# A transformer block: VectorE's weight splits queued behind the copies that TensorE waits for, and latent attention in another order

## The chip, the cores and the metric

One core of a Trainium2 chip (trn2). Five engines work from queues of their own: TensorE (PE: matmuls and transposes into PSUM), VectorE (DVE), ScalarE (ACT), GpSimd (POOL) and SyncE (SP, which here issues the transfers of the weights). An engine takes its queue strictly in order, so an instruction that waits holds up all that stand behind it on its engine. The metric is the device time of one execution in microseconds: the median of three is 914.4 us (912.42 to 914.48).

## The reference, cut to what matters

Two blocks on 256 tokens of width 1024, all in float32. The first has a layer with a bidirectional mLSTM beside spatial gating, and a layer with latent attention. Each is followed by a feed-forward layer of width 4096. The second block has chunked attention and SwiGLU. The part that is re-ordered is the latent attention:

```python
    cq, ckv, kr = jnp.split(h @ w_in, [Q_LORA, Q_LORA + KV_LORA], axis=-1)       # 384, 256, 32
    q = (rms_norm(cq, q_g) @ w_uq).reshape(bsz, seq, C_HEADS, C_NOPE + C_ROPE)   # 16 heads of 64 + 32
    kv = (rms_norm(ckv, kv_g) @ w_ukv).reshape(bsz, seq, C_HEADS, C_NOPE + C_V)  # 64 + 64
    q_rope = apply_rope(q[..., C_NOPE:], cos, sin)
    k_rope = apply_rope(kr[:, :, None, :], cos, sin)
    ...
    s = jnp.einsum("bqhd,bkhd->bhqk", qblk, kf) * scale
    pr = jax.nn.softmax(s, axis=-1)
    o = jnp.einsum("bhqk,bkhd->bqhd", pr, v)
    return o @ w_out
```

The outer parts are `x + ab_mixer(...)` and `x + mla_mixer(...)`, each followed by `x + square(relu(rms_norm(x) @ w1)) @ w2`.

## The kernel before, in words

**Products.** TensorE works on a reduced float32 type (fp32r), and each float32 factor is split into a high and a low part. A product of 128x128 weights with 128x256 activations takes three matmuls (`three`, L369 to L374): high weight by high activation (L371), high weight by low activation (L372), low weight by high activation (L373).

**The weight stream.** Weights arrive as chunks of up to 128x2048 (1 MB), listed in `items` in order of use. `Stream` transfers them into a ring of three `raw` buffers. For each chunk ScalarE writes the high part `whi` (L149), and VectorE, or GpSimd for the chunks named in `ON_POOL`, writes the low part `wlo = raw - whi` (L152), mostly in two halves of 128x1024. Four pairs `whi`/`wlo` are held. These steps are put into the program a few at a time between matmuls, by a list of deferred work (`Later`), and a scheduler then settles the order of each engine's queue. `issue_after(x)` tells it that an instruction has to stand behind x; no wait on the chip comes with it. `S.behind` already uses this for `whi` on ScalarE.

**Activations.** A finished sum is added into `head`, the residual (L497). ScalarE rounds it to `xh`, VectorE forms `xl` (L303), and the next layer's matmuls need both.

**Latent attention (L900 to L1202).** In this stretch TensorE's order is the order of the code. The latents `ch`/`cl` (`cl`: L949) are projected by `q_rope` (rotary parts of the queries, 18 matmuls), `q_nope` (L1006 copies the result to `qn`, 18 matmuls), `k_nope` (L1011 scales it into `kn`, 12 matmuls) and `values` (6 matmuls of 128x512, ScalarE writes `v`, L1023). The 16 heads are worked in four groups. `sc(a)` makes the scores of four heads (L1071, L1076). `exps(a)` takes their maxima on VectorE (L1086, L1087), and ScalarE exponentiates in two pairs of heads, with the row sums (L1090). `nrm(j)` takes reciprocals (L1097) and scales one head of the pair on VectorE, the other on GpSimd (L1100). `tr(j)` transposes a pair on TensorE (L1114), copied to `pT` (L1116). `pv(j)` multiplies by the values (L1126). Projections, transposes (j up to 3) and `pv` results share one ring of four PSUM banks (`mmt`); the scores have another (`auxt`). A product can start only when the bank it gets, used four products earlier, has been read. Then follows `c_out`, the output projection.

Of the kernel before, what the change touches and what calls it, by code (L numbers as in the profile page):

```python
# [10 lines left out]
F32 = mybir.dt.float32  # L11
# [39 lines left out]
def spread(ap, axis, n):  # L51

    shape = list(ap.shape)
    shape[axis] = n
    return ap.broadcast_to(shape)
# [44 lines left out]
class Stream:  # L100
# [4 lines left out]

    def __init__(self, tc, later, raw_pool, hl_pool, items, on_pool=()):
        nc = tc.nc
        self.tc, self.behind = tc, None
        self.on_pool = set(on_pool)
        self.nc, self.later, self.raw_pool, self.hl_pool, self.items = nc, later, raw_pool, hl_pool, items  # L110
        self.raw, self.hl, self.todo = {}, {}, {}
        self.n_dma = self.n_split = self.n_use = self.n_plan = 0
# [18 lines left out]
    def split(self):  # L131

        i = self.n_split
        if i >= len(self.items):
            return
        self.n_split += 1
        w = self.items[i].shape[-1]
        r = self.raw.pop(i)
        hi = self.hl_pool.tile([P, BLK * P], F32R, tag="whi", name="whi")
        lo = self.hl_pool.tile([P, BLK * P], F32R, tag="wlo", name="wlo")  # L140
        self.hl[i] = (hi, lo)
        n = self.parts(i)
        parts = [slice(j * w // n, (j + 1) * w // n) for j in range(n)]

        eng = self.nc.gpsimd if i in self.on_pool else self.nc.vector

        def h(s):
            with self.tc.issue_after(self.behind.ins) if self.behind else nullcontext():
                self.nc.scalar.activation(hi[:, s], r[:, s], AF.Copy)  # L149

        def l(s, last):
            eng.tensor_tensor(lo[:, s], r[:, s], hi[:, s].bitcast(F32), op=ALU.subtract)  # L152
            if last:
                self.dma()

        steps = []
        for n, s in enumerate(parts):
            steps.append(lambda s=s: h(s))
            steps.append(lambda s=s, last=n == len(parts) - 1: l(s, last))
        self.todo[i] = steps  # L160
# [33 lines left out]
def block_kernel(ctx, tc, a, out):  # L194
# [46 lines left out]
    items = []  # L241
    on_pool = []
    for n in ("w_va", "w_qk01", "w_qk23", "w_vb", "w_u", "w_oa", "w_ab_out", "w1_0", "w2_0", "w_cin",
              "w_uq", "w_uk", "w_uv", "w_uq2", "w_c_out", "w1_1", "w2_1", "w_qk2", "w_v2",
              "w_o2", "w_gu4", "w_gu", "w_down"):
        first = len(items)
        items += [a[n][i] for i in range(a[n].shape[0])]
        if n == "w_cin":
            items[-1] = items[-1][:, 0:KB * P]
        on_pool += [first + i for i in ON_POOL.get(n, ())]  # L250
# [49 lines left out]
    def split_x(k, src, scale):  # L300

        act.activation(xh[:, k], src, AF.Copy, scale=scale)
        dve.scalar_tensor_tensor(xl[:, k], src, scale, xh[:, k].bitcast(F32), op0=ALU.mult,  # L303
                                 op1=ALU.subtract)

    def split_lo(k, g):
        dve.scalar_tensor_tensor(xl[:, k], x[:, k], col(g, k), xh[:, k].bitcast(F32), op0=ALU.mult,
# [590 lines left out]
    with tc.tile_pool(name="mla", bufs=1) as ap:  # L898
# [43 lines left out]
        def c_evac(m, ps):  # L942
            for i in range(ps.shape[1]):
                j = m + i
                kv = j < 2
                g = col("kv_g", j) if kv else col("q_g", j - 2)
                sq = tmp.tile([P, T], F32, tag="sq", name="sq", bufs=3)
                act.activation(ch[:, j], ps[:, i], AF.Copy, scale=g)
                dve.scalar_tensor_tensor(cl[:, j], ps[:, i], g, ch[:, j].bitcast(F32), op0=ALU.mult,  # L949
                                         op1=ALU.subtract)  # L950
                act.activation(sq, ps[:, i], AF.Square)
                key = "kv" if kv else "q"
                if j in (0, 2):
                    state[key] = sq
                else:
                    n = mp.tile([P, T], F32, tag="sqa", name="sqa", bufs=2)
                    pool.tensor_tensor(n, state[key], sq, op=ALU.add)
                    state[key] = n
                if j == 1:
                    later(4.4, rkv_chain)  # L960
                if j == 4:
                    later(6.0, rq_chain)
# [18 lines left out]
        def tiles(w, b0, h, l, nk, n):  # L981

            ps = mmt().rearrange("p (a b) -> p a b", a=2)
            wh, wl = w
            for i in range(n):
                for k in range(nk):
                    s = slice((b0 + i * nk + k) * P, (b0 + i * nk + k + 1) * P)
                    three(ps[:, i], wh[:, s], wl[:, s], h[k], l[k], k == 0, k == nk - 1)
            return ps
# [3 lines left out]
        def q_rope(w, g):  # L993

            ps = tiles(w, 6 * g, CK[2:5], CL[2:5], 3, 2)
            qs = qr[:, 2 * g:2 * g + 2]
            q2 = mp.tile([P, 2, T], F32, tag="q2", name="q2")
            act.activation(qs, ps, AF.Copy)
            for i in range(2):
                dve.stream_shuffle(q2[:, i], qs[:, i], SHUF)  # L1000
                pool.tensor_tensor(qs[:, i], qs[:, i], cosT, op=ALU.mult)
                dve.tensor_tensor(q2[:, i], q2[:, i], sinT, op=ALU.mult)
                dve.tensor_tensor(qs[:, i], qs[:, i], q2[:, i], op=ALU.add)

        def q_nope(w, g):
            dve.tensor_copy(qn[g], tiles(w, 6 * (g % 2), CK[2:5], CL[2:5], 3, 2))  # L1006

        def k_nope(w, g):
            ps = tiles(w, 4 * g, CK[0:2], CL[0:2], 2, 2)
            for i in range(2):  # L1010
                dve.tensor_tensor(kn[g][:, i], ps[:, i], rbc[1], op=ALU.mult)  # L1011

        def values(w, n, tt):
            ts = slice(tt * P, (tt + 1) * P)
# [27 lines left out]
        act.activation(kr4, thin(wkr, "c_norm"), AF.Copy)  # L1042

        w = S.get()
        q_rope(w, 0)
        key_rope()
        q_rope(w, 1)
# [2 lines left out]
        q_nope(w, 0)  # L1050
        wk = S.get()
        k_nope(wk, 0)
        q_nope(w, 1)
        S.done(held=2)
        k_nope(wk, 1)
        wv = S.get()
        later.flush()
        mpc.__exit__(None, None, None)
        mpc = tc.tile_pool(name="mls", bufs=2)
# [20 lines left out]
        def exps(a, pss):  # L1080
            for p in range(2):
                mx = mp.tile([P, 2, 2], F32, tag="mx", name="mx", bufs=3)
                sm = mp.tile([P, 2, 2], F32, tag="sm", name="sm", bufs=8)
                prs = [mp.tile([P, 2, T], F32, tag="pr", name="pr", bufs=16) for _ in range(2)]
                for i in range(2):
                    dve.tensor_reduce(mx[:, i], pss[2 * p + i], axis=AX, op=ALU.max)  # L1086
                dve.tensor_tensor(mx, mx, spread(nsrq.unsqueeze(1), 1, 2), op=ALU.mult)  # L1087
                for i in range(2):
                    for qt in range(2):
                        S.behind = act.activation(prs[i][:, qt], pss[2 * p + i][:, qt], AF.Exp,  # L1090
                                                  scale=srq[:, qt:qt + 1], bias=mx[:, i, qt:qt + 1],
                                                  accum_out=sm[:, i, qt:qt + 1])
                st_p[2 * a + p] = (prs, sm)

        def nrm(j):
            prs, sm = st_p[j]
            dve.reciprocal(sm, sm)  # L1097
            for i in range(2):
                for qt in range(2):
                    (pool if i else dve).tensor_scalar(prs[i][:, qt], prs[i][:, qt], sm[:, i, qt:qt + 1], None,  # L1100
                                                       op0=ALU.mult)
# [5 lines left out]
        def tr(j):  # L1107
            prs, sm = st_p.pop(j)
            st_t[j] = []
            for i in range(2):  # L1110
                ps = bank(j).rearrange("p (a b) -> p a b", a=2)
                for kt in range(2):
                    for qt in range(2):
                        pe.transpose(ps[:, kt, qt * P:(qt + 1) * P], prs[i][:, qt, kt * P:(kt + 1) * P], ident)  # L1114
                pT = pT_[(2 * j + i) % 4]
                (act.activation(pT, ps, AF.Copy) if i and j > 3 else dve.tensor_copy(pT, ps))  # L1116
                st_t[j].append(pT)
            later.tick(0.9)

# [17 lines left out]
            dve.tensor_tensor(yl[j], o[:, 0:T], yh[j].bitcast(F32), op=ALU.subtract)  # L1137

        sc(0)
        w = S.get()  # L1140
        q_nope(w, 2)
        k_nope(wk, 2)
        values(wv, 0, 0)
        values(wv, 0, 1)
        nrm(0)
        nrm(1)
        sc(1)
        q_nope(w, 3)
        S.done(held=3)
        k_nope(wk, 3)  # L1150
        S.done(held=2)
        values(wv, 1, 0)
        values(wv, 1, 1)
        S.done()
        nrm(2)
        nrm(3)
        sc(2)
        tr(0)
        tr(1)
        pv(0)  # L1160
        tr(2)
        pv(1)
        nrm(4)
        nrm(5)
        sc(3)
        tr(3)
        pv(2)
        pv(3)
        nrm(6)
        nrm(7)  # L1170
# [455 lines left out]
```

## Time and profile before

| What | Value |
|---|---|
| median of three runs | 914.4 us (912.42 to 914.48) |
| the profiled execution | 912.91 us, of which the span from first to last instruction is 911.2 us |
| TensorE busy | 881.4 us, 97% of the span, 6744 matmuls |
| VectorE, ScalarE, GpSimd busy | 578.1, 470.7, 277.1 us |
| chain that ended last | TensorE 83%, VectorE 9% (its L152 alone 3%) |
| mean granted clock of TensorE | 0.986 of full speed |

TensorE is the bound almost everywhere, so an edit matters only where it changes TensorE's idle time or its clock. The list of waits says what TensorE stood idle for; the timeline of an engine says what it did then; the table by stretches shows its clock (1.00 is 2.4 GHz, 0.50 is 1.2 GHz).

### The profile page before, as it was taken

What the parts mean: (1) busy time and instruction counts of PE and PEld (TensorE: products, weight loads), DVE (VectorE), ACT (ScalarE), POOL (GpSimd) and SP (SyncE); (2) the same over time, 40 slices, a digit from 0 to 9 for tenths busy, and PEclk for the clock granted to TensorE, in tenths of its full rate; (3) what the DMA queues carried; (4) which work ended last, traced back from release to release, by engine and by line L of the source; (5) the groups of instructions that cost most, each with busy time, mean ns of one, the idle gap of its engine ahead of it and who ended that gap; (6) DMA issues with size and microseconds to landing.
All of it is one profiled execution on the core that took longest, in us unless ns stands there. A gap on an engine that the chain in (4) does not pass through costs nothing.

```text
span 911.2 us, 16494 instructions
## 1 busy us (share of the span) xinstructions
PE 881.4 (97%) x6744; PEld 820.8 (90%) x6744; DVE 578.1 (63%) x921; ACT 470.7 (52%) x824; POOL 277.1 (30%) x281
## 2 busy tenths in 40 slices
PE   8899999999999988798999999999999999999997
PEld 7789999999999987588999999999877789999885
DVE  7697889555555467846755555548783766666442
ACT  6685568555444353555655544425375765444331
POOL 6877733333011254656333201110147000000000
PEclk9999999999999999899999999999999999999999
DMA  8543454655554422324555555559342565555521
GB/s 307 187 165 120 164 180 170 226 186 185 186 185 163 168 82 94 104 82 172 193 191 185 186 185 186 185 187 276 140 140 96 192 242 187 186 186 193 191 78 47
DMA packets 25579, 154.38 MB, mean 169 GB/s; under 512 B 2736, under 2 KB 5216, under 8 KB 8224
## 3 DMA queue, kind: packets, MB, share of 16 engines
q1 hardware_dynamic: 22176, 148.18, 46.2%
q10 hardware_dynamic: 3040, 4.36, 2.0%
q8 instruction: 53, 0.87, 0.4%
q0 software_dynamic: 288, 0.79, 0.3%
q14 instruction: 22, 0.18, 0.1%
HBM read 152.25 MB, written 1.07 MB: 168 GB/s over the span
## 4 chain that ended last, share of the span: by engine, by line
PE 83%; DVE 9%; issue 2%; ACT 2%; DMA 1%; POOL 1%; SPq 0%; DVEq 0%; POOLq 0%; ACTq 0%
PE mm L371 20%; PE mm L372 20%; PE mm L373 20%; DVE wlo L152 3%; PE aux L469 2%; PE aux L468 2%; PE aux L470 2%; DVE acc L715 2%; PE mm L433 2%; PE mm L435 2%; PE mm L434 2%; PE mm L468 1%; PE mm L470 1%; PE mm L469 1%; DMA raw<-in_w_qk_dram 1%
## 5 line engine op out<-in xcount | busy, mean ns | idle before, releaser
L149 ACT ACTIVATE whi<-raw 128x1024 fp32r<-128x1024 f32 (+3 forms) x318 | 285.4, 951 | 236.4 <-PE mm L372 152.4
L152 DVE TENSOR_TENSOR wlo<-raw,whi 128x1024 fp32r<-128x1024 f32 (+2 forms) x254 | 307.0, 1245 | 118.7 <-ACT whi L149 117.1
L372 PE MATMUL mm<-xl,whi 128*128 128x256 f32 x1080 | 301.4, 280 | 2.4 <-DVE xl L303 2.4
L371 PE MATMUL mm<-xh,whi 128*128 128x256 f32 x1080 | 301.7, 282 | 0.0
L373 PE MATMUL mm<-xh,wlo 128*128 128x256 f32 x1080 | 301.0, 279 | 0.0
L372 PEld LDWEIGHTS mm<-xl,whi 128*128 128x128 f32 x1080 | 204.0, 189 | 3.1 <-DVE xl L303 2.8
L373 PEld LDWEIGHTS mm<-xh,wlo 128*128 128x128 f32 x1080 | 205.9, 191 | 0.0
L371 PEld LDWEIGHTS mm<-xh,whi 128*128 128x128 f32 x1080 | 202.8, 189 | 0.6 <-issue 0.4
L371 PE MATMUL mm<-hh,whi 128*128 128x256 f32 x512 | 143.9, 281 | 0.0
L372 PE MATMUL mm<-hl,whi 128*128 128x256 f32 x512 | 143.9, 281 | 0.0
L373 PE MATMUL mm<-hh,wlo 128*128 128x256 f32 x512 | 143.9, 281 | 0.0
L373 PEld LDWEIGHTS mm<-hh,wlo 128*128 128x128 f32 x512 | 98.3, 192 | 0.0
L371 PEld LDWEIGHTS mm<-hh,whi 128*128 128x128 f32 x512 | 96.1, 188 | 0.0
L372 PEld LDWEIGHTS mm<-hl,whi 128*128 128x128 f32 x512 | 96.1, 188 | 0.0
L152 POOL TENSOR_TENSOR wlo<-raw,whi 128x512 fp32r<-128x512 f32 (+2 forms) x64 | 84.4, 1344 | 27.6 <-ACT whi L149 27.5
L522 POOL TENSOR_TENSOR fu<-ft 128x512 f32<-128x512 f32 (+1 forms) x36 | 54.8, 1524 | 122.2 <-ACT ft L520 114.5
L316 POOL TENSOR_TENSOR s_acc<-s_acc,sq 128x256 f32<-128x256 f32 x37 | 43.7, 1187 | 153.6 <-ACT sq L315 142.9
L1225 POOL TENSOR_TENSOR r<-v,nhalf 128x1 f32<-128x1 f32 x4 | 2.2, 559 | 193.5 <-DVE v L1224 193.5
L433 PE MATMUL mm<-whi,xh 128*128 128x512 f32 x96 | 39.5, 430 | 0.6 <-ACT whi L149 0.5
L434 PE MATMUL mm<-wlo,xh 128*128 128x512 f32 x96 | 38.2, 401 | 1.6 <-DVE wlo L152 1.6
L523 DVE TENSOR_TENSOR hl<-fu,hh 128x512 fp32r<-128x512 f32 (+1 forms) x36 | 24.1, 675 | 23.4 <-POOL fu L522 23.4
L435 PE MATMUL mm<-whi,xl 128*128 128x512 f32 x96 | 38.1, 400 | 0.6 <-DVE xl L1434 0.6
(371 smaller groups left out, 1324.0 us busy)
## 6 DMA issues: line engine op xcount, KB each, us to landing
raw<-in_w_dram SPq DMA_DIRECT2D x64, 1024.0 KB, 4.9
raw<-in_w_gu_dram SPq DMA_DIRECT2D x22, 1024.0 KB, 4.8
raw<-in_w_qk_dram SPq DMA_DIRECT2D x12, 1024.0 KB, 5.1
raw<-in_w_down_dram SPq DMA_DIRECT2D x11, 1024.0 KB, 4.8
raw<-in_w_ab_out_dram SPq DMA_DIRECT2D x4, 1024.0 KB, 5.0
raw<-in_w_c_out_dram SPq DMA_DIRECT2D x4, 1024.0 KB, 4.8
raw<-in_w_v_dram SPq DMA_DIRECT2D x4, 1024.0 KB, 5.8
raw<-in_w_o_dram SPq DMA_DIRECT2D x4, 1024.0 KB, 4.8
```

What stands on the lines that cost most here:

```text
L149: self.nc.scalar.activation(hi[:, s], r[:, s], AF.Copy)
L152: eng.tensor_tensor(lo[:, s], r[:, s], hi[:, s].bitcast(F32), op=ALU.subtract)
L316: state["sum"] = (dve if k == last else pool).tensor_tensor(acc, acc, sq, op=ALU.add)
L371: pe.matmul(ps, wh, h, start=start, stop=False)
L372: pe.matmul(ps, wh, l, start=False, stop=False)
L373: pe.matmul(ps, wl, h, start=False, stop=stop)
L433: pe.matmul(pss[tt], h[k][:, ts], wh[:, s], start=k == 0, stop=False)
L434: pe.matmul(pss[tt], h[k][:, ts], wl[:, s], start=False, stop=False)
L435: pe.matmul(pss[tt], l[k][:, ts], wh[:, s], start=False, stop=k == nk - 1)
L468: pe.matmul(ps, h[k][:, ts], wh[:, ns], start=k == 0, stop=False)
L469: pe.matmul(ps, h[k][:, ts], wl[:, ns], start=False, stop=False)
L522: pool.tensor_tensor(u[:, 0:g], t[:, 0:g], t[:, 0:g], op=ALU.mult)
```

## The change

It has three parts. First, `S.low` remembers the latest of certain VectorE instructions, and a split on VectorE is put behind it in the queue. Second, the chunk `w_uv` (values) comes ahead of `w_uq` and `w_uk`. Third, the calls of latent attention stand in another order. Lines of the changed kernel are two to six higher than before.

```diff
         def l(s, last):
-            eng.tensor_tensor(lo[:, s], r[:, s], hi[:, s].bitcast(F32), op=ALU.subtract)
+            on_dve = i not in self.on_pool and self.low
+            with self.tc.issue_after(self.low.ins) if on_dve else nullcontext():
+                eng.tensor_tensor(lo[:, s], r[:, s], hi[:, s].bitcast(F32), op=ALU.subtract)
...
-              "w_uq", "w_uk", "w_uv", "w_uq2", "w_c_out", "w1_1", "w2_1", "w_qk2", "w_v2",
+              "w_uv", "w_uq", "w_uk", "w_uq2", "w_c_out", "w1_1", "w2_1", "w_qk2", "w_v2",
...
-        dve.scalar_tensor_tensor(xl[:, k], src, scale, xh[:, k].bitcast(F32), op0=ALU.mult,
+        S.low = dve.scalar_tensor_tensor(xl[:, k], src, scale, xh[:, k].bitcast(F32), op0=ALU.mult,
...
-                dve.scalar_tensor_tensor(cl[:, j], ps[:, i], g, ch[:, j].bitcast(F32), op0=ALU.mult,
+                S.low = dve.scalar_tensor_tensor(cl[:, j], ps[:, i], g, ch[:, j].bitcast(F32), op0=ALU.mult,
...
-                dve.tensor_tensor(qs[:, i], qs[:, i], q2[:, i], op=ALU.add)
+                S.low = dve.tensor_tensor(qs[:, i], qs[:, i], q2[:, i], op=ALU.add)
...
-            dve.tensor_copy(qn[g], tiles(w, 6 * (g % 2), CK[2:5], CL[2:5], 3, 2))
+            S.low = dve.tensor_copy(qn[g], tiles(w, 6 * (g % 2), CK[2:5], CL[2:5], 3, 2))
...
-                dve.tensor_tensor(kn[g][:, i], ps[:, i], rbc[1], op=ALU.mult)
+                S.low = dve.tensor_tensor(kn[g][:, i], ps[:, i], rbc[1], op=ALU.mult)
...
-                dve.tensor_tensor(mx, mx, spread(nsrq.unsqueeze(1), 1, 2), op=ALU.mult)
+                S.low = dve.tensor_tensor(mx, mx, spread(nsrq.unsqueeze(1), 1, 2), op=ALU.mult)
...
-                (act.activation(pT, ps, AF.Copy) if i and j > 3 else dve.tensor_copy(pT, ps))
+                if i and j > 3:
+                    act.activation(pT, ps, AF.Copy)
+                else:
+                    S.low = dve.tensor_copy(pT, ps)
```

The order of the calls, where `nrm`, which issues nothing on TensorE, is left out:

```text
before: q_rope 0,1  q_nope 0  k_nope 0  q_nope 1  k_nope 1  sc 0  q_nope 2  k_nope 2  values 0,0 0,1  sc 1
        q_nope 3  k_nope 3  values 1,0 1,1  sc 2  tr 0,1  pv 0  tr 2  pv 1  sc 3  tr 3  pv 2,3  c_out
now:    values 0,0 0,1 1,0 1,1  q_rope 0,1  q_nope 0  k_nope 0  sc 0  q_nope 1  k_nope 1  q_nope 2  sc 1
        q_nope 3  k_nope 2  tr 0,1  pv 0  sc 2  k_nope 3  tr 2  pv 1  tr 3  pv 2  sc 3  pv 3  c_out
```

How the queues move shows at three places. First, VectorE at the end of the first layer. `wlo_1448` is the low part of the last chunk of that layer's output projection, `ybl` are low parts of activations that its matmuls need, and the sums `mm_1443` and `mm_1512` are its last two. Before:

```order
L786 TENSOR_TENSOR ybl_153<-yt_1122,ybh_152 128x256
L786 TENSOR_TENSOR ybl_153<-yt_1163,ybh_152 128x256
L793 SCALAR_TENSOR_TENSOR yt_1187<-aux_1184,head_78,bsr_150 128x256
L793 SCALAR_TENSOR_TENSOR yt_1210<-aux_1207,head_78,bsr_150 128x256
L816 TENSOR_TENSOR sg_158<-mm_1221,rbc0_86 128x512
L786 TENSOR_TENSOR ybl_153<-yt_1187,ybh_152 128x256
L152 TENSOR_TENSOR wlo_1448<-raw_1199,whi_1447 128x1024
L804 SCALAR_TENSOR_TENSOR yt_1258<-aux_1255,head_78,sg_158 128x256
L152 TENSOR_TENSOR wlo_1448<-raw_1199,whi_1447 128x1024
L786 TENSOR_TENSOR ybl_153<-yt_1210,ybh_152 128x256
```

And now, later in VectorE's queue:

```order
L499 TENSOR_TENSOR head_78<-mm_1314,head_78 128x256
L305 SCALAR_TENSOR_TENSOR xl_93<-head_78,xh_92 128x256 x2
L499 TENSOR_TENSOR head_78<-mm_1443,head_78 128x256 x2
L305 SCALAR_TENSOR_TENSOR xl_93<-head_78,xh_92 128x256 x2
L154 TENSOR_TENSOR wlo_1448<-raw_1199,whi_1447 128x1024 x2
L305 SCALAR_TENSOR_TENSOR xl_93<-head_78,xh_92 128x256 x2
L154 TENSOR_TENSOR wlo_1517<-raw_1291,whi_1516 128x1024 x2
L154 TENSOR_TENSOR wlo_1525<-raw_1362,whi_1524 128x1024 x2
L499 TENSOR_TENSOR head_78<-mm_1512,head_78 128x256 x2
```

The split that stood ahead of a `ybl` has moved behind the residual of `mm_1443` and four `xl`.

Second, TensorE's queue at the same place, now, from the first matmul of `mm_1512` on, which follows the last of `mm_1443` (the weights 1516 and 1524 are the next layer's):

```order
L373 MATMUL mm_1512<-yah_1114,whi_1447 128x256
L374 MATMUL mm_1512<-yah_1114,whi_1447 128x256
L373 MATMUL mm_1597<-xh_92,whi_1516 128x256
L374 MATMUL mm_1597<-xl_93,whi_1516 128x256
L373 MATMUL mm_1604<-xh_92,whi_1516 128x256
L374 MATMUL mm_1604<-xl_93,whi_1516 128x256
L373 MATMUL mm_1608<-xh_92,whi_1524 128x256
L374 MATMUL mm_1608<-xl_93,whi_1524 128x256
L375 MATMUL mm_1512<-yah_1114,wlo_1448 128x256
```

Before, the product by `wlo_1448` stood third; now eight matmuls stand ahead of it.

Third, VectorE in latent attention. Before, from the copy of the last `q_nope` (`qn`) to the first transposes (`pT`):

```order
L1006 COPY qn<-mm 128x512
L1100 TENSOR_SCALAR pr<-pr,sm 128x256 x2
L152 TENSOR_TENSOR wlo<-raw,whi 128x1024
L1011 TENSOR_TENSOR kn<-mm,rbc_87 128x256 x2
L152 TENSOR_TENSOR wlo<-raw,whi 128x1024 x3
L1086 TENSOR_REDUCE mx<-aux 128x2 x3
L1087 TENSOR_TENSOR mx<-mx,nsrq 128x4
L1086 TENSOR_REDUCE mx<-aux 128x2
L1087 TENSOR_TENSOR mx<-mx,nsrq 128x4
L1116 COPY pT_3645<-mm 128x512
L1116 COPY pT_3646<-mm 128x512
```

Now, from the split ahead of the third `qn` to the second `pT` (`sm` is the row sums, whose reciprocal waits for the exponentials):

```order
L154 TENSOR_TENSOR wlo<-raw,whi 128x1024
L1008 COPY qn<-mm 128x512
L154 TENSOR_TENSOR wlo<-raw,whi 128x1024
L1089 TENSOR_REDUCE mx<-aux 128x2 x4
L1090 TENSOR_TENSOR mx<-mx,nsrq 128x4 x2
L1100 RECIPROCAL sm<-sm 128x4
L1008 COPY qn<-mm 128x512
L1103 TENSOR_SCALAR pr<-pr,sm 128x256 x2
L1013 TENSOR_TENSOR kn<-mm,rbc_87 128x256 x2
L1122 COPY pT_3645<-mm 128x512
L1100 RECIPROCAL sm<-sm 128x4
L1122 COPY pT_3646<-mm 128x512
```

No split stands between the scores and `pT` any more; the last `qn`, a `kn` and the second `pT` now stand behind a reciprocal.

## Rows read from the trace of the kernel before

**Rows 1.** TensorE's waits over the whole span: total us, times, longest.

```profile
PE mm L1126 <- DVE pT L1116: 5.5, 2, 4.3
PE mm L372 <- DVE xl L303: 2.4, 2, 1.8
PE aux L1071 <- DVE kn L1011: 2.4, 1, 2.4
PE mm L372 <- DVE cl L949: 2.3, 1, 2.3
...
PE mm L372 <- DVE ybl L786: 0.7, 1, 0.7
```

**Rows 2.** TensorE's timeline in latent attention: start, duration, operation, count, [idle before, releaser].

```profile
326.06 0.38 PE L371 MATMUL mm<-ch,whi 128*128 128x256 f32 x1
...
346.01 2.88 PE L1071 MATMUL aux<-kn,qn 64*128 64x256 f32 x16 [2.39 <-DVE kn L1011]
...
350.64 0.38 PE L371 MATMUL mm<-ch,whi 128*128 128x256 f32 x1
...
354.15 0.39 PE L1019 MATMUL mm<-whi,ch 128*128 128x512 f32 x1
...
356.99 2.06 PE L1071 MATMUL aux<-kn,qn 64*128 64x256 f32 x16
...
360.06 0.38 PE L371 MATMUL mm<-ch,whi 128*128 128x256 f32 x1
...
369.41 1.09 PE L1114 MATMUL mm<-ident,pr 128*128 128x128 f32 x8
...
390.34 0.38 PE L371 MATMUL mm<-yh,whi 128*128 128x256 f32 x1
```

**Rows 3.** Stretches: length, busy of PE, PEld, DVE, ACT, POOL, granted clock, DMA.

```profile
330.00:333.00 3.00, 2.95 (x14) 2.95 (x15) 0.00 (x0) 1.06 (x4) 1.46 (x2) 0.50 0.01 4
347.00:350.00 3.00, 3.00 (x22) 2.04 (x22) 2.64 (x8) 0.00 (x0) 0.25 (x1) 0.50 0.99 404
423.00:426.00 3.00, 2.78 (x23) 2.78 (x24) 3.00 (x8) 2.74 (x7) 2.77 (x4) 1.00 0.92 382
```

**Rows 4.** VectorE's timeline between the first layer and its feed-forward layer.

```profile
124.40 0.74 DVE L497 TENSOR_TENSOR head<-mm,head 128x256 f32<-128x256 f32 x2
125.06 1.35 DVE L303 SCALAR_TENSOR_TENSOR xl<-head,xh 128x256 fp32r<-128x256 f32 x2
126.34 2.89 DVE L152 TENSOR_TENSOR wlo<-raw,whi 128x1024 fp32r<-128x1024 f32 x2
```

**Rows 5.** VectorE's timeline ahead of the second feed-forward layer.

```profile
417.80 2.27 DVE L152 TENSOR_TENSOR wlo<-raw,whi 128x1024 fp32r<-128x1024 f32 x1
```

**Rows 6.** GpSimd's timeline in the same stretch.

```profile
415.17 6.04 POOL L152 TENSOR_TENSOR wlo<-raw,whi 128x512 fp32r<-128x512 f32 x4 [3.74 <-ACT whi L149]
```

**Rows 7.** VectorE's timeline in latent attention.

```profile
338.49 2.04 DVE L152 TENSOR_TENSOR wlo<-raw,whi 128x768 fp32r<-128x768 f32 x1
...
345.54 0.74 DVE L1011 TENSOR_TENSOR kn<-mm,rbc 128x256 f32<-128x256 f32 x2
...
347.23 0.68 DVE L1006 COPY qn<-mm 128x512 f32<-128x512 f32 x1
...
350.74 2.48 DVE L1086 TENSOR_REDUCE mx<-aux 128x2 f32<-128x512 f32 x4 [1.10 <-PE aux L1076]
...
355.71 0.18 DVE L1097 RECIPROCAL sm<-sm 128x4 f32<-128x4 f32 x1 [0.60 <-ACT pr L1090]
355.93 0.84 DVE L1100 TENSOR_SCALAR pr<-pr,sm 128x256 f32<-128x256 f32 x2
...
367.58 1.21 DVE L152 TENSOR_TENSOR wlo<-raw,whi 128x1024 fp32r<-128x1024 f32 x1
```

**Rows 8.** ScalarE's timeline in latent attention.

```profile
337.86 0.59 ACT L998 ACTIVATE qr<-mm 128x512 f32<-128x512 f32 x1
353.38 0.57 ACT L1090 ACTIVATE pr<-aux,mx,srq 128x256 f32<-128x256 f32 x1 [14.94 <-PE mm L373]
```

More of the change, by code (lines that the diff above doesn't have):

```diff
@@ L107, in __init__ @@
         nc = tc.nc
-        self.tc, self.behind = tc, None
+        self.tc, self.behind, self.low = tc, None, None
         self.on_pool = set(on_pool)
@@ L302, in split_x @@
         act.activation(xh[:, k], src, AF.Copy, scale=scale)
-        dve.scalar_tensor_tensor(xl[:, k], src, scale, xh[:, k].bitcast(F32), op0=ALU.mult,
-                                 op1=ALU.subtract)
+        S.low = dve.scalar_tensor_tensor(xl[:, k], src, scale, xh[:, k].bitcast(F32), op0=ALU.mult,
+                                         op1=ALU.subtract)
     def split_lo(k, g):
@@ L948, in c_evac @@
                 act.activation(ch[:, j], ps[:, i], AF.Copy, scale=g)
-                dve.scalar_tensor_tensor(cl[:, j], ps[:, i], g, ch[:, j].bitcast(F32), op0=ALU.mult,
-                                         op1=ALU.subtract)
+                S.low = dve.scalar_tensor_tensor(cl[:, j], ps[:, i], g, ch[:, j].bitcast(F32), op0=ALU.mult,
+                                                 op1=ALU.subtract)
                 act.activation(sq, ps[:, i], AF.Square)
@@ L1044, in block_kernel @@
         w = S.get()
+        for n in range(2):
+            for tt in range(2):
+                values(w, n, tt)
+        S.done()
+        w = S.get()
         q_rope(w, 0)
@@ L1052, in block_kernel @@
         k_nope(wk, 0)
[L1053 to L1056, printed above, removed]
         later.flush()
@@ L1139, in block_kernel @@
         sc(0)
+        q_nope(w, 1)
+        S.done(held=2)
+        k_nope(wk, 1)
         w = S.get()
         q_nope(w, 2)
-        k_nope(wk, 2)
-        values(wv, 0, 0)
-        values(wv, 0, 1)
         nrm(0)
@@ L1148, in block_kernel @@
         q_nope(w, 3)
-        S.done(held=3)
-        k_nope(wk, 3)
         S.done(held=2)
-        values(wv, 1, 0)
-        values(wv, 1, 1)
-        S.done()
+        k_nope(wk, 2)
+        tr(0)
+        tr(1)
+        pv(0)
         nrm(2)
@@ L1157, in block_kernel @@
         sc(2)
-        tr(0)
-        tr(1)
-        pv(0)
+        k_nope(wk, 3)
+        S.done()
         tr(2)
         pv(1)
+        tr(3)
+        pv(2)
         nrm(4)
@@ L1165, in block_kernel @@
         sc(3)
-        tr(3)
-        pv(2)
         pv(3)
```

## The prediction

> **What bounds the kernel now.** I read the busy shares first: TensorE works 97% of the span, so the most that any order of the other engines can give back is its idle time, some 30 us, and what its clock loses after an idle stretch. The list of TensorE's waits comes next [rows 1]. The reader is to see five lines that name VectorE: copies and low parts of activations that were late, 13.3 us together, of which 12.6 lie in latent attention and ahead of the feed-forward layer behind it. Then TensorE's timeline of latent attention [rows 2]: it runs from 326.06 to the first matmul of the output projection at 390.34, which is 64.3 us. Its work at full clock I add up from the same rows. Thirty matmuls of 128x256 take 354.15 - 350.64 = 3.51, so 0.117 each, and the 156 of the query and key tiles 18.2. Two value tiles take 356.99 - 354.15 = 2.84, so four take 5.7. A group of scores takes 360.06 - 356.99 = 3.07, so four take 12.3. Four transposed pairs at 1.09 and four value products, which I put at the same length, take 8.7. Small broadcasts and column sums I estimate at 0.8 together, seven matmuls' worth. That is 45.7 us; some 19 are lost to waits and clock. Last the clock [rows 3]: it stood at 0.50 for three microseconds behind the idle 2.3 (`cl`) and behind the idle 2.39 (`kn`), but at 1.00 behind the idle 1.8 (`xl`, at 423). The scores at 346.01 took 4.63 in place of 3.07 for it [rows 2]. So I price a fall of the clock at 1.6, and count one where a wait is as long as those two.
>
> **End of the first layer: +3.0.** Removed is the wait on `ybl`, 0.7 [rows 1], since the split that stood ahead of it moves. But that split is the low half of the chunk that `mm_1512` needs, and it now stands behind the residual of `mm_1443` and two `xl` that depend on it. Before, nothing waited here. Now, counted from the end of `mm_1443`, which the residual at 124.40 follows: to the first `xl` 0.66, from there to the next instruction 1.28, and half of the pair of splits 1.45 [rows 4]. The matmul by `wlo_1448` is free to start 3.4 later, and TensorE has eight matmuls of 0.117 ahead of it, 0.9. It idles 2.5. At the shortest durations (0.41 for each of four, taken from the 0.74 of a pair in [rows 7], and 1.21 for the split [rows 7]) it would be 1.9. A fall of the clock would add 1.6; I take 1.2 of it, since the shorter wait is like the one after which the clock stayed. The second half of the split and the splits of 1517 and 1525 that follow end under the 5.5 us (48 matmuls by 0.117) of `mm_1512`. Sum: -0.7 + 2.5 + 1.2 = +3.0, from +1.2 to +3.4.
>
> **Ahead of the second feed-forward layer: -2.4.** Before, a split of 2.27 at 417.80 stood between two residuals [rows 5], and TensorE waited 1.8 and 0.6 for `xl` [rows 1]. Now all eight `xl` stand ahead of the four splits on VectorE. The first two chunks of that layer come from GpSimd, which ended at 421.2 [rows 6]. TensorE was busy for 2.78 of the three microseconds from 423 [rows 3], so it began again at 423.2 and had stood since 421.4: GpSimd was through by then. The splits now put last belong to chunks that are used after the 96 matmuls of the first two, 11 us on; at 2.27 each the first pair takes 4.5, so they are hidden. Bounds: -1.2, if GpSimd ends a microsecond later, to -2.4.
>
> **Latent attention: -1.3.** The layout runs from 326.1 in the clock of the trace of before. The waits on `cl` and its half clock go, about 4, but other ones come.
>
> *To the first scores.* Values 5.7, then 66 matmuls of 0.117 (three query tiles and one key tile), 7.7, and 0.8 of small products end at 340.3. The first `kn` is not there yet. The second rotary tile ends at 336.9; its copy by ScalarE (0.59 [rows 8]) stands behind four value copies and splits and ends about 338.3. Behind it VectorE has two shuffles, two products, three sums at about 0.42 each (a pair of such size takes 0.74 [rows 7], one after another a little more), `qn` 0.68 and `kn` 0.74: 4.4, more where GpSimd runs beside, so between 342.7 and 345.2. I take 343.6. TensorE idles 3.3, and the scores take 4.6 at half clock: 348.2. Before, they ended at 350.6, but two more projections (3.5) were done and the values (5.7) were not.
>
> *To the second scores.* TensorE has 48 matmuls, to 353.8. VectorE's three splits and a sum end at 347.0, under the scores. The maxima take 2.48 to 350.8; from the exponentials' first instruction to the reciprocal it is 355.71 - 353.38 = 2.33 [rows 7, 8], which gives 353.3. Then `qn` 0.68, a scaling 0.84 and `kn` 0.74 [rows 7]: 355.6. TensorE idles 1.8, where before it had no wait; the scores end at 358.7.
>
> *The transposes.* VectorE does a reciprocal and scaling to 356.6, then split 1.21, `qn`, split 1.21. One of the two falls beside GpSimd's scaling, for which I add 1.0 (the split of 768 columns took 2.04 against 0.91, three quarters of 1.21 [rows 7]): 360.7. The maxima end at 363.2, the reciprocal at 365.7, the last `qn` at 366.4, `kn` at 368.0, the two `pT` at 368.7 and 369.5. TensorE, after 30 matmuls and a pair of transposes, stands at 363.3. The next transpose needs the bank of the last `qn`: idle 3.1, then 1.0 for the bank of `kn`, then 0.9 for the second `pT`. With half a clock behind it the third scores end at 375.4. So the split has left the path, and a reciprocal that waits for exponentials has taken its place.
>
> *To the end.* VectorE's two splits and `yh`, `yl` are through at 375.0, below the scores. Maxima of a pair (1.3), exponentials 2.33, scaling, `kn`: 380.8; two `pT` to 382.4. TensorE has key tile, transposes and a value product to 379.0, then waits 1.8, 0.2 and 0.3, then value product, scores, value product: 387.7, and 0.5 for a bank of the output projection. For a fall of the clock at the 1.8 I take half, 0.8. The end is 389.0, against 390.34: -1.3. Between its bounds lie `kn` at 342.7 or 345.2, the slow split or none, a fall of the clock or none, and the splits at double length (below): -6 to +4.
>
> A rule of the Trainium skill bears on the double length. The row shows one split of 1024 columns at 2.27 [rows 5] while GpSimd worked from 415.17 to 421.2 [rows 6], against 1.21 alone [rows 7]. The page "GPSIMD Engine Reference", section "8. Key points", says that GpSimd shares its SBUF interfaces with VectorE, with contention where a VectorE instruction has two SBUF inputs; a split has two. By that rule it speaks against the change to put splits where GpSimd scales probabilities; by the row alone the sum would hold one slow split, as above.
>
> **The sum.** +3.0 - 2.4 - 1.3 = -0.7. The second block's splits move too, but where the trace shows no wait of TensorE, so I put that at 0 (plus or minus 0.5). From the profiled execution's 912.9 it gives 912.2. The median of the runs lies 1.5 above the profiled execution, so the forecast is 913.7: no change that can be told.
>
> **Rivals.**
> *The short chains hold (0.32).* The rotary chain runs without GpSimd beside it (342.7: -0.9), no split is slowed (-1.0), the clock falls neither at the end of the first layer (-1.2) nor at the late transposes (-0.8). That is -3.9: 909.8. For it speaks that the late waits are close to the 1.8 after which the clock stayed; against it that the same chain before had two slow splits in it.
> *The splits run at double length (0.22).* Seven splits now stand ahead of maxima. At the three before the first maxima 3.4 of added time, of which 1.3 is covered by the scores: +2.1. At the second +1.0 more, at the third +1.7. That is +4.8 on the forecast: 918.5. It decides where GpSimd is at work in more than one of these places; against it speaks that the splits ahead of the first maxima end 1.2 before the scores do, and that GpSimd scales only one head of each pair.
> *The change does not do what it says (0.06).* The scheduler leaves the queue of latent attention in effect as it was, and only the layer ahead of the feed-forward gains: -2.4, so 912.0. Against it speak the queues, in which the splits do move.
>
> **How the numbers follow.** The forecast has 0.40. A change under 0.3% (2.7 us, 911.7 to 917.1) cannot be told from none. Nearly all of the first rival is faster, with a tenth of the forecast: 0.36. Nearly all of the second is slower, with a tenth of the forecast: 0.26. The rest, 0.38, is the same. The range reaches from below the first rival, 908.5, to the second, 918.5. The forecast's own range is 911 to 917.
>
> **What would show it.** In the list of TensorE's waits the lines for `cl` and `xl` are gone, and `pT` is under 2. A new wait of about 2.5 for `wlo` stands near 124, and the clock behind it at 0.50. In latent attention waits on `kn` or on banks that VectorE reads stand ahead of the first scores (3), the second scores (2) and the second transposes (3). The output projection starts some 2 us after where it stood, for the 2.3 lost at the first layer. The forecast is wrong if the layout's reciprocals come earlier than I have them, or if splits beside GpSimd stand on the path in more than one place.

## The result, and the profile after

The changed kernel takes 899.2 us (median of 4, 897.5 to 902.2) against 914.4 (912.4 to 914.5): a ratio of 0.984, with a 95% interval of 0.981 to 0.987. I had forecast 913.7, and 908.5 as the low end. The profiled execution took 897.51 us, with a span of 895.8.

The first thing to read is on top of the page. TensorE's busy time was 881.4 of a span of 911.2; now it is this, of 895.8 (page, engines' busy time):

```profile
PE 865.6 (97%) x6744; PEld 805.2 (90%) x6744; DVE 573.8 (64%) x921; ACT 469.6 (52%) x824; POOL 268.5 (30%) x281
```

The idle time is 29.8 before and 30.2 after. So TensorE waits as long as it did, and the same 6744 matmuls take 15.8 us less. A part of that is less time at half clock (mean clock 0.986 before, 0.990 after), and the larger part lies where nothing was changed. These are two stretches of 20 us in the two feed-forward layers of the first block (length, busy us and matmuls of TensorE, granted clock, DMA), before:

```profile
240.00:260.00 20.00, 20.00 (x172) 1.00 0.57 186
520.00:540.00 20.00, 20.00 (x172) 1.00 0.57 204
```

and after:

```profile
240.00:260.00 20.00, 20.00 (x178) 1.00 0.51 199
520.00:540.00 20.00, 20.00 (x179) 1.00 0.59 211
```

The reader is to see a full TensorE at a granted clock of 1.00 in all four, and 172 matmuls of 128x256 against 178 or 179. From start to start it is 0.1178 us before and 0.1133 after. I call this the pitch. It goes over at a sharp place. In the trace of before it is 0.1133 from 129.4 to 149.6 and 0.1178 behind this (TensorE's timeline):

```profile
149.71 0.40 PE L345 MATMUL aux<-dg,ones_r 128*128 128x256 f32 x2
```

It stays so up to the column sums at 314.6, and again from 445.0 to 609.9. These two matmuls broadcast the row scale of the layer, as the high and the low part of a diagonal (`spread_rows`). In the changed kernel they are no longer neighbours:

```profile
153.76 0.28 PE L347 MATMUL aux<-dg,ones_r 128*128 128x256 f32 x1
...
155.51 0.39 PE L347 MATMUL aux<-dg,ones_r 128*128 128x256 f32 x1
```

Behind each the pitch is back at 0.1133 within three matmuls. The diagonal's low part now comes later on VectorE: in this layer it is through at 155.46, where it was through at 148.76 before. So the scheduler put the two apart, a side effect of the splits' new places, which nothing in the change speaks of.

Of the waits that [rows 1] shows, those for `xl`, `cl`, `ybl` and `pT` are gone or under 0.2. The list after (total us, times, longest):

```profile
PE aux L1074 <- DVE kn L1013: 4.8, 2, 3.5
PE mm L375 <- DVE wlo L154: 2.4, 1, 2.4
PE mm L1117 <- DVE qn L1008: 2.2, 1, 2.2
PE mm L1117 <- DVE kn L1013: 2.2, 1, 2.2
...
PE mm L1117 <- POOL pr L1103: 0.8, 1, 0.8
```

The new wait at the end of the first layer stands where I had put it, and half a clock behind it (timeline, then the table by stretches, TensorE alone):

```profile
126.89 0.48 PE L375 MATMUL mm<-yah,wlo 128*128 128x256 f32 x1 [2.43 <-DVE wlo L154]
```

```profile
127.00:130.00 3.00, 3.00 (x15) 0.50 0.35 52
...
343.00:346.00 3.00, 3.00 (x20) 0.59 0.03 5
366.00:369.00 3.00, 3.00 (x12) 0.50 0.00 0
```

Latent attention after, to be held against [rows 2]:

```profile
324.61 0.50 PE L1021 MATMUL mm<-whi,ch 128*128 128x512 f32 x1
...
342.57 3.41 PE L1074 MATMUL aux<-kn,qn 64*128 64x256 f32 x16 [3.50 <-DVE kn L1013]
...
354.02 2.00 PE L1074 MATMUL aux<-kn,qn 64*128 64x256 f32 x16 [1.31 <-DVE kn L1013]
...
363.92 0.65 PE L1117 MATMUL mm<-ident,pr 128*128 128x128 f32 x4 [2.22 <-DVE qn L1008]
365.33 0.63 PE L1117 MATMUL mm<-ident,pr 128*128 128x128 f32 x4 [0.75 <-POOL pr L1103]
365.89 2.58 PE L1132 MATMUL mm<-pT,v 128*64 128x256 f32 x8
...
377.62 1.31 PE L1117 MATMUL mm<-ident,pr 128*128 128x128 f32 x8 [2.22 <-DVE kn L1013]
...
383.91 0.38 PE L373 MATMUL mm<-yh,whi 128*128 128x256 f32 x1
```

From its first matmul to that of the output projection it takes 59.3, against 64.3. Put together from the starts of TensorE's matmuls at the borders of the stages:

| Stage, up to | before | after | difference | forecast |
|---|---|---|---|---|
| column sums of the first feed-forward layer (end of the first layer) | 140.05 | 144.11 | +4.1 | +3.0 |
| last matmul of that layer | 309.88 | 308.28 | -5.7 | 0 |
| start of latent attention | 326.06 | 324.61 | +0.2 | 0 |
| start of the output projection | 390.34 | 383.91 | -5.0 | -1.3 |
| first matmul of the second layer's down projection | 514.58 | 502.82 | -5.3 | -2.4 |
| its last | 604.91 | 589.74 | -3.4 | 0 |
| end | 911.2 | 895.8 | -0.2 | 0 |

### The profile page after: what moved, and what is told of

It is laid out like the page before. It is cut to its first block, busy times and chain, and to the rows that moved or that the text cites. A ratio compares the mean times of both kernels' runs of the same rounds, so it can differ in the third digit from the quotient of the medians.

```text
span 895.8 us, 16451 instructions
## 1 busy us (share of the span) xinstructions
PE 865.6 (97%) x6744; PEld 805.2 (90%) x6744; DVE 573.8 (64%) x921; ACT 469.6 (52%) x824; POOL 268.5 (30%) x281
## 4 chain that ended last, share of the span: by engine, by line
PE 83%; DVE 8%; ACT 3%; issue 2%; DMA 2%; POOL 0%; SPq 0%; DVEq 0%; POOLq 0%; ACTq 0%
PE mm L373 20%; PE mm L375 20%; PE mm L374 20%; PE aux L472 2%; PE aux L471 2%; PE aux L470 2%; PE mm L435 2%; DVE acc L717 2%; DVE wlo L154 2%; PE mm L437 2%; PE mm L436 2%; ACT whi L149 1%; ACT pr L1093 1%; PE aux L1074 1%; PE mm L470 1%
## 5 line engine op out<-in xcount | busy, mean ns | idle before, releaser
L149 ACT ACTIVATE whi<-raw 128x1024 fp32r<-128x1024 f32 (+2 forms) x318 | 285.3, 951 | 225.7 <-PE mm L374 140.2
L375 PEld LDWEIGHTS mm<-xh,wlo 128*128 128x128 f32 x1080 | 203.5, 189 | 0.0
L373 PE MATMUL mm<-hh,whi 128*128 128x256 f32 x512 | 141.3, 276 | 0.0
L374 PE MATMUL mm<-hl,whi 128*128 128x256 f32 x512 | 141.3, 276 | 0.0
L375 PE MATMUL mm<-hh,wlo 128*128 128x256 f32 x512 | 141.3, 276 | 0.0
L375 PEld LDWEIGHTS mm<-hh,wlo 128*128 128x128 f32 x512 | 96.1, 188 | 0.0
L154 POOL TENSOR_TENSOR wlo<-raw,whi 128x512 fp32r<-128x512 f32 (+2 forms) x64 | 81.8, 1305 | 21.2 <-ACT whi L149 21.1
L318 POOL TENSOR_TENSOR s_acc<-s_acc,sq 128x256 f32<-128x256 f32 x37 | 40.4, 1098 | 147.8 <-ACT sq L317 147.1
```

The lines of the kernel that those rows point to most:

```text
L318: state["sum"] = (dve if k == last else pool).tensor_tensor(acc, acc, sq, op=ALU.add)
L373: pe.matmul(ps, wh, h, start=start, stop=False)
L374: pe.matmul(ps, wh, l, start=False, stop=False)
L375: pe.matmul(ps, wl, h, start=False, stop=stop)
```

## The experiments

Each was timed in rounds beside the kernel before on one chip; a ratio is to those runs. The edits are cut to the lines that matter, with helper calls written out. Two stretches of each trace tell the pitch: at 240 to 260 the first feed-forward layer, at 520 to 540 the second.

**The pair put apart, in the kernel before.** Nothing else differs.

```diff
-        for i in range(2):
-            pe.matmul(ps[:, 0:T], ones_r, dg[:, i]..., start=i == 0, stop=i == 1)
-        S.behind = act.activation(dst, ps[:, 0:T], AF.Copy)
+        one(0)                      # first matmul
+        later(1.0, rest)            # second matmul and the copy, twelve matmuls later
```

> The kernel before, with one edit: in both feed-forward layers of the first block the two matmuls of the broadcast (high and low part of the diagonal) are no longer neighbours in TensorE's queue; twelve matmuls stand between them. Theory: the two traces differ by 12.4 us in the pitch of TensorE's plain matmuls, 0.1178 us in both feed-forward layers before and 0.1133 after, at the same granted clock; before, the pitch rises at the pair and stays, and with the pair apart it does not. Then 914.4 - 12.4 = 902.0 (900 to 904), pitch 0.1133 behind the broadcast. Rival 1, the pitch goes with where the queues of VectorE or the tiles stand, not with the pair: 914 (913 to 916), pitch 0.1178.

903.9 us (903.1 to 904.3), ratio 0.989 (0.987 to 0.992), so 9.9 us faster:

```profile
240.00:260.00 20.00, 20.00 (x179) 1.00 0.63 211
520.00:540.00 20.00, 20.00 (x179) 1.00 0.59 206
```

The code of the splits and of latent attention is that of before, and its waits are there too (`pT` 5.5, `cl` 2.3). Rival 1 falls. In its trace the two layers, measured from the column sums on, are 12.0 us shorter; its first layer took 2.2 us longer in that execution with the same code, all of it ahead of 100 us. (By 100 us the other traces here stand 0.2 to 2.7 behind that of before, so a trace tells less about that stretch than about the later ones.)

**The pair put together, in the changed kernel.**

```diff
-                bcast(rbc[0], r_col[1], dt=5.0)
+                bcast(rbc[0], r_col[1], dt=9.0)
```

> The changed kernel, with one edit: in both feed-forward layers of the first block the broadcast is issued 4 us later, by when both halves of the diagonal are there, and its two matmuls stand side by side in TensorE's queue as they did before the change. Theory of the pair: pitch 0.1178 behind it, and 899.2 + 12 = 911 (909 to 913). Rival 1, the pitch goes with the splits' place on VectorE, which is as in the changed kernel: 899 (897 to 902), pitch 0.1133.

909.7 us (908.3 to 912.1), ratio 0.996 (0.994 to 0.998): of the 15 us some 4 are left.

```profile
240.00:260.00 20.00, 20.00 (x172) 1.00 0.58 209
520.00:540.00 20.00, 20.00 (x172) 1.00 0.29 106
```

**The splits alone.** `S.low` as in the change, the order of chunks and calls as before.

```diff
-              "w_uv", "w_uq", "w_uk", "w_uq2", ...
+              "w_uq", "w_uk", "w_uv", "w_uq2", ...
```

> The splits behind the copies as in the changed kernel, but the chunks and the calls of latent attention in the order of before. The pair of broadcast matmuls stands apart here, as in the changed kernel. Theory of the pair: -12.4 for the pitch, +4.1 at the end of the first layer, -2.4 ahead of the second feed-forward layer, and in latent attention some of the 5.0 that the changed kernel gains there, I say 2: 901.7 (899 to 904). Rival 1 (the pitch goes with the splits on VectorE) says the same here. Rival 2, the pitch goes with the order of the chunks in latent attention and the tiles that this moves: 912.

908.6 us, but from 901.3 to 910.2; ratio 0.993 (0.990 to 0.996). The profiled execution had the first layer at 0.1133 and the second at 0.1178, though its two matmuls stand apart there, as in the changed kernel. The first had to wait:

```profile
441.09 0.39 PE L347 MATMUL aux<-dg,ones_r 128*128 128x256 f32 x1 [0.48 <-DVE dg L340]
...
442.02 0.31 PE L347 MATMUL aux<-dg,ones_r 128*128 128x256 f32 x1
```

So it is not the neighbourhood alone. From the end of the first feed-forward layer to the output projection this kernel takes 0.7 more than before (trace). Of that, 3.4 is lost ahead of latent attention, where TensorE waits 1.7 for `sqa`, which GpSimd writes, and runs at a granted clock of 0.58 from 324 to 327. In latent attention it takes 2.7 less, near the 2 that I had said: the wait for `cl` is 0.9 there, and a new one of 2.1 is for `wlo`.

**The order alone.** Chunks and calls as in the change, without `issue_after` for the splits.

```diff
-            with self.tc.issue_after(self.low.ins) if on_dve else nullcontext():
-                eng.tensor_tensor(...)
+            eng.tensor_tensor(...)
```

> Chunks and calls of latent attention in the new order, the splits on VectorE where they were before. The pair of broadcast matmuls stands together, as before. Theory of the pair: pitch 0.1178 in both feed-forward layers, no stall at the end of the first layer, the 2.4 for the activations ahead of the second feed-forward layer still there, and in latent attention a part of the 5.0, I say 2: 912 (909 to 915). Rival 2 (the pitch goes with the order of the chunks): 900.

915.2 us (914.0 to 917.5), ratio 1.002 (1.001 to 1.003). The pitch is 0.1178 in both layers. In the same stretch it takes 0.9 more than before, and in latent attention alone 0.3 less, not 2; the splits stand ahead of the keys (TensorE's waits):

```profile
PE aux L1073 <- DVE kn L1012: 7.6, 2, 4.4
PE mm L1116 <- DVE kn L1012: 3.1, 1, 3.1
```

By these traces, one of each, either part alone costs a little from the end of the feed-forward layer to the output projection, and both together give 4.8. Over that stretch the gain is neither's own.

**The last chunk of the first layer split early**, in the changed kernel:

```diff
-            on_dve = i not in self.on_pool and self.low
+            on_dve = i not in self.on_pool and i not in self.free and self.low    # free: that chunk
```

> The changed kernel, but the last chunk of the first layer's output projection is split on VectorE where the scheduler put it before the change, not behind the copies. Theory: the wait of 2.43 us for its low part and the half clock behind it go, 4.1 us in all against the trace of before: 895.2 (893 to 897) if the pitch behind both broadcasts stays 0.1133. Rival: the time is given back in the next stage, since the splits of the feed-forward layer's first chunks come later by the 2.4 us that this split takes: 899.

897.4 us (895.3 to 902.8), ratio 0.983 (0.980 to 0.987). The wait for `wlo` is gone from the trace; latent attention gained 3.8 in place of 5.0, since the scheduler moved other instructions too. Against the changed kernel the intervals overlap.

**One more alone, and three in a row**, in the kernel before:

```diff
+            pe.matmul(auxt()[:, 0:T], ones_r, dg[:, 0]..., start=True, stop=True)
```

> The kernel before with extra matmuls of the broadcast's shape that write a bank nobody reads. In the first feed-forward layer the pair stands side by side as before, and one more follows alone some 20 matmuls later. In the second, three stand side by side. Theory A, the last interruption decides: the lone one brings the pitch back from 0.1178 to 0.1133 in the first layer. Theory B, the pair fixes it until another kind of instruction comes: 0.1178 to the end of that layer. For three in a row I have no theory that says; the pair suggests 0.1178. A and slow: 914 - 6 = 908; B and slow: 914; A and fast: 902.

901.5 us (899.5 to 903.1), ratio 0.987 (0.985 to 0.989). Where the extra ones stand:

```profile
151.10 0.40 PE L346 MATMUL aux<-dg,ones_r 128*128 128x256 f32 x2
...
153.81 0.28 PE L346 MATMUL aux<-dg,ones_r 128*128 128x256 f32 x1
```

From 151.3 to 153.7 the pitch is 0.1175, behind 153.8 it is 0.1133 to the layer's end: the last interruption decides, as theory A had it. Three in a row in the second layer gave 0.1133, against what I had guessed. A matmul more in each layer made the kernel faster by 11 us.

**Near, and later**, in the kernel before: the pair three matmuls apart in the first layer, together but nine matmuls later in the second.

```diff
-                bcast(rbc[0], r_col[1], dt=5.0)
+                bcast(rbc[0], r_col[1], dt=6.0)          # second layer
```

> The kernel before. In the first feed-forward layer the two matmuls of the broadcast stand three matmuls apart, in the second side by side but 9 matmuls later than before. If it is the neighbourhood that raises the pitch, the first layer runs at 0.1133 (the records of the changed kernel show a lone one costing its bubble over three matmuls, so three may just do) and the second at 0.1178: 908 (906 to 910). If it is the place in the stream, the second may be fast: 902; if three matmuls do not part them: 914.

907.8 us (904.6 to 910.4), ratio 0.993 (0.991 to 0.996), with the first layer at 0.1133 and the second at 0.1178: the place in the stream is not what counts.

```profile
240.00:260.00 20.00, 20.00 (x179) 1.00 0.60 211
520.00:540.00 20.00, 20.00 (x172) 1.00 0.62 207
```

**Four in a row, and one of other weights beside the first**, in the kernel before:

```diff
+            for _ in range(2):                                                        # first layer
+                pe.matmul(auxt()[:, 0:T], ones_r, dg[:, 0]..., start=True, stop=True)
+            pe.matmul(auxt()[:, 0:T], dg[:, 0, 0], xh[:, 0], start=True, stop=True)   # second
```

> The kernel before with extra matmuls that write a bank nobody reads. In the first feed-forward layer four of the broadcast's shape stand side by side, in the second one with other weights (the diagonal by an activation) beside the first of the broadcast, whose second follows twelve matmuls later. So far one and three brought the pitch of 0.1133 and two 0.1178. If an even number raises it: 0.1178 in the first layer; if only two do: 0.1133. If it needs the same weights twice, the second layer is fast; if any two foreign matmuls do it, it would be slow for those twelve and fast behind the next. 908 in the one case, 902 in the other.

909.0 us (907.6 to 910.1), ratio 0.995 (0.994 to 0.997). Four raise the pitch as two do:

```profile
240.00:260.00 20.00, 20.00 (x172) 1.00 0.55 191
520.00:540.00 20.00, 20.00 (x179) 1.00 0.59 205
```

In the second layer the twelve matmuls between the pair of unlike weights and the next ran at 0.1136. So in this trace two foreign matmuls in a row did not raise the pitch when their weights differed.

**The changed kernel and the early chunk once more, on one chip.**

> The changed kernel itself, on the same chip as the next run: 899 (897 to 902).

> The version with the early last chunk once more, beside the changed kernel on one chip. Its trace had no wait at the end of the first layer (-3.9 against the changed kernel) and 1.1 more in latent attention, since the scheduler also moved other instructions: 2.7 below the changed kernel, 896.5 (895 to 899). Rival: the two cannot be told apart, because each execution differs by as much in the first hundred microseconds.

898.8 (896.5 to 906.4) and 902.0 (897.1 to 902.5), ratios 0.986 and 0.986: the rival was right that they can't be told apart. In the profiled executions its reason was not the one, since by 100 us they stand only 0.5 apart. In that of the second the first feed-forward layer went at 0.1178, where the same kernel had 0.1133 the time before. A wait fell on the second matmul of the broadcast:

```profile
152.93 0.39 PE L351 MATMUL aux<-dg,ones_r 128*128 128x256 f32 x1 [0.23 <-DVE dg L345]
```

```profile
240.00:260.00 20.00, 20.00 (x172) 1.00 0.51 193
```

One program at both pitches: so no placement of tiles and no order of a queue decides it alone.

**Three in a row with nothing to wait for**, in both versions: the broadcast 4 us later, one unread matmul more beside its two.

```diff
+        if odd:
+            pe.matmul(auxt()[:, 0:T], ones_r, dg[:, 0]..., start=True, stop=True)
...
-                bcast(rbc[0], r_col[1], dt=5.0)
+                bcast(rbc[0], r_col[1], dt=9.0, odd=True)
```

> The version with the early last chunk; in both feed-forward layers of the first block the broadcast is issued 4 us later, when both halves of the diagonal are there, and a third matmul of its shape, which writes a bank nobody reads, stands beside its two. Three brought the pitch of 0.1133, and with nothing to wait for there the pitch cannot go over to 0.1178 from one execution to the next, as it did in the first layer in the second trace of the early version. 896 in all executions (894 to 898). Rival: the pitch is chance, and executions at 902 or above come here too.

> The changed kernel with the same three matmuls side by side and the later broadcast. Pitch 0.1133 in both layers in all executions: 899 (897 to 901), with none at 906 as one of the changed kernel was. Rival: 911 as with the pair together, or executions at both.

895.7 us (895.2 to 896.8), ratio 0.981 (0.979 to 0.983), with the early chunk, and 897.9 (896.3 to 900.5), ratio 0.982 (0.980 to 0.985), without. The second is the kernel with the pair together (909.7) with one unread matmul more in each layer, and both layers of its trace are at 0.1133:

```profile
240.00:260.00 20.00, 20.00 (x179) 1.00 0.59 211
520.00:540.00 20.00, 20.00 (x179) 1.00 0.52 196
```

The first has the lowest median here, though its interval overlaps that of the changed kernel (0.981 to 0.987). Its executions lie within 1.6 us, where those of the changed kernel in one series lay within 10. The pitch is not all that scatters: the second's profiled execution took 900.5 at 0.1133 in both layers, with its first layer 2.3 us longer than in the first trace of the changed kernel.

## Why the prediction was wrong

The step that failed is the first: "the most that any order of the other engines can give back is its idle time, some 30 us, and what its clock loses". I took the pitch of the plain matmuls for a constant (0.117, from thirty of them in [rows 2]) and never measured it in the feed-forward layers. It was 0.1178 in both, while it was 0.1133 in the same layers ahead of the broadcast and in the long plain stretch of the second block (748 to 842). The order of TensorE's queue shows the pair of the broadcast parted. That is 12.0 us of the 15.4 by the trace of the pair put apart, and 9.9 by its times; putting the pair together took 10.5 back. So most of the gain was luck: the change was not made for it.

The rest of the difference between the traces is near -3, where the sum said -0.7.

- *End of the first layer*, +3.0: +4.1. The wait of 2.5 was 2.43, and the clock fell for the whole time (0.50 from 127 to 130), of which I had counted three quarters. By the starts of matmuls the two cost 4.8, where I had 3.7, and the missing wait for `ybl` gave back 0.9. Right in kind and place, above my upper bound of +3.4.
- *Ahead of the second feed-forward layer*, -2.4: right. The waits on `xl` are gone; of the -5.3 of that row of the table 2.6 is pitch (what the kernel with the pair apart gains from the column sums to that row) and 2.7 the rest.
- *Latent attention*, -1.3: -5.0. The layout held up to the second scores: it had the first at 17.5 and the second at 29.5 after the start, and they stand at 18.0 and 29.4. Behind them four terms were too large. The slow split (1.0) did not come: the split at 355.29 took 1.21. The wait of 0.9 for the second `pT` was 0, as its reciprocal had nothing left to wait for. Behind the late transposes the clock stayed (0.8), and no bank of the output projection was late (0.5). That is 3.2 of the 3.7. The mechanism, reciprocals behind exponentials in place of splits, is in the list of waits: `qn` and `kn` in front of transposes, 2.2 each.
- *The clock.* I had counted a fall where a wait is as long as 2.3. These traces do not bear that out: the length alone did not tell. Behind the wait of 1.8 for `xl` the clock stayed at 1.00 before [rows 3], and behind the same wait of 1.8 it was 0.50 in the kernel with the pair apart (first line); TensorE had been busy for 1.39 and 1.16 of the three microseconds ahead. In the changed kernel it was 0.50 at 366, behind waits of 2.2 and 0.8, and 1.00 at 378, behind one of 2.2 (second line).

```profile
420.00:423.00 3.00, 3.00 (x16) 0.50 0.85 330
```

```profile
378.00:381.00 3.00, 2.97 (x25) 1.00 0.02 5
```

- *The fast rival* named two of these terms (the split, the late fall) and had 909.8, without the pitch. *The slow rival*, splits at double length beside GpSimd, did not happen. The rule of the Trainium skill that I had weighed ("GPSIMD Engine Reference", section "8. Key points") names contention where VectorE's instruction has two SBUF inputs, and not which engine is held up. The trace agrees with the contention, and GpSimd was the one that took longer. VectorE's timeline and GpSimd's, after:

```profile
355.29 1.21 DVE L154 TENSOR_TENSOR wlo<-raw,whi 128x1024 fp32r<-128x1024 f32 x1
```

```profile
354.59 2.70 POOL L1103 TENSOR_SCALAR pr<-pr,sm 128x256 f32<-128x256 f32 x2 [0.25 <-DVE sm L1100]
363.39 1.92 POOL L1103 TENSOR_SCALAR pr<-pr,sm 128x256 f32<-128x256 f32 x2 [6.10 <-DVE sm L1100]
```

The split ran at the length that it has with GpSimd idle (1.21 at 326.57 before), in the middle of GpSimd's scaling. But the two scalings took 2.70, where the next two, with no split beside them, took 1.92. The trace of before had shown this. I had called the split at 367.58 in [rows 7] alone, but two scalings stood beside it, and they took 2.98:

```profile
366.52 2.98 POOL L1100 TENSOR_SCALAR pr<-pr,sm 128x256 f32<-128x256 f32 x2 [0.20 <-PE mm L1021]
```

The price of 1.0 came from splits that stood beside GpSimd's splits. There too it fell on either engine: VectorE's took 2.27 in [rows 5], but one took 1.22 at 334.47 of the same trace (first line, VectorE), where GpSimd's took longer (5.20 for three):

```profile
334.47 1.22 DVE L152 TENSOR_TENSOR wlo<-raw,whi 128x1024 fp32r<-128x1024 f32 x1
334.53 5.20 POOL L152 TENSOR_TENSOR wlo<-raw,whi 128x512 fp32r<-128x512 f32 x3 [2.43 <-ACT whi L149]
```

What stays open is why the pitch has two values. Shown is that in these layers it goes over at an interruption of the plain stream and stays until the next; that two or four matmuls of the broadcast in a row brought 0.1178 in the feed-forward layers of all the traces here, and one or three without a wait 0.1133; and that it was 0.1178 behind the two broadcasts before which the timeline shows a wait (0.48 and 0.23), in the second case in a program that had 0.1133 without the wait. The number of foreign matmuls is no general rule: the four column sums behind the first feed-forward layer left 0.1133 in the kernel with the pair apart (310.7) and brought 0.1178 in the changed kernel (312.8), with no wait in either. What in TensorE keeps this was not found.

## What to carry to other kernels

Where one engine is the bound, measure the distance from start to start of its plain instructions in every long stage, and compare the stages, before counting waits: a difference of 4% there gave 12 us, where the waits that this change was about gave some 3. Two edits of a queue may each cost in a stretch and together gain there, so read them apart and together. And when a faster version's executions scatter, look for one stage that runs at two paces before blaming the clock.

## What the runs showed of the hardware that was not expected

- TensorE's stream of weight loads and matmuls of 128x256 has two steady pitches, 0.1133 and 0.1178 us, at a granted clock of 1.00. Over one feed-forward layer the slower one costs 6 us. Adding one matmul that nobody reads to each of the two layers made the kernel before faster (901.5 against 912.9) and the changed kernel with the pair together too (897.9 against 909.7, in two series).
- Where a VectorE split of 1024 columns ran beside GpSimd's work, either engine could be the one that took longer: the split 2.27 in place of 1.21 (417.80, before), or two of GpSimd's scalings 2.70 in place of 1.92 (354.59, after) while the split took 1.21.
- Behind TensorE's wait of 1.8 for the same tile the granted clock was 1.00 in one trace (423 to 426, before) and 0.50 in another (420 to 423, pair apart).
